# An FFN's modulation products tied to its activation products on VectorE

## The chip, the core and the metric

The kernel runs on one core of one Trainium2 chip. The metric is the device time of one execution in microseconds (us), first instruction to last and what lies around it. Three runs of the kernel before gave 2541.69 to 2549.84 us, with a median of 2549.1 us.

## What is computed

A transformer of four layers (an FFN, a mixer, an FFN each), followed by a second block of a hybrid mixer, a cross attention and one more FFN, on 256 tokens of width 1024, all in float32. The modulation of layer i is a matrix-vector product with `w_mod`, and depends on the conditioning vector alone, not on the tokens:

```python
cond = jax.nn.silu(c)
for i in range(DEPTH):                                   # DEPTH = 4
    mod = (cond @ w_mod[i] + b_mod[i]).reshape(-1, N_SUBLAYERS, N_MOD, D_MODEL)
    x = _sublayer(x, ffn_0, mod[:, 0], ...)
    x = _sublayer(x, mixer_i, mod[:, 1], ...)
    x = _sublayer(x, ffn_1, mod[:, 2], ...)

def _swiglu(h, w_in, w_out):
    gate, up = jnp.split(h @ w_in, 2, axis=-1)
    return (jax.nn.silu(gate) * up) @ w_out

def _sublayer(x, fn, mod_j, g, b, weight):
    shift, scale, gate = mod_j[:, 0, None, :], mod_j[:, 1, None, :], mod_j[:, 2, None, :]
    y = fn(x * (1 + scale) + shift)
    return _layernorm(DEEPNORM_ALPHA * x + weight * gate * y, g, b)
```

## The kernel before, in words

**A product in three matmuls.** Each float32 operand is split into a high and a low part, and a product is three matmuls: high by high, high by low, low by high. A weight arrives as a transfer of 1 MB into a `raw` tile (three of these tiles exist, `NR = 3`). ScalarE writes the high parts `whi` (L219), VectorE the low parts `wlo` in three chunks for each 128x1024 tile (L222).

**An FFN.** Its 2816 hidden columns are worked in 11 blocks (b = 0 to 10) of 256, for two halves of the tokens (t = 0, 1). FFNs are counted from 0 here; FFN 0, 2, 4, 6 are the first ones of the layers, 1, 3, 5, 7 the second ones, 8 the last of the program. The steps are:

- I(t,b): the transfer of the block's weights (three of 1 MB, at t = 0), 24 matmuls into `hid{b}t{t}`, the silu `sg` on ScalarE (L596), the activation product `ac` on VectorE (L599), and then some steps of a background generator (`tick`).
- T(t,b): two transposes of `ac` on TensorE (L263), the high part `ah` on ScalarE (L608), the low part `al` on VectorE (L609).
- O(t,b): 12 matmuls into the accumulators y0 (t = 0) or y1 (t = 1): L623 and L624 take `ah`, L625 takes `al`.

The order in which the program writes the steps of the middle blocks is I(0,b) O(0,b-1) I(1,b) T(0,b) O(1,b-1) T(1,b). After the last block, `post_ln` adds the residual and normalises y0, then y1 (L511 to L524), and what it has normalised, `r`, is transposed for the next sublayer (the L263 rows with `r`); the next sublayer's first matmuls are into `pa`, `pd` or `pz`.

**The modulation.** The background generator (`mod_dot`) computes the modulation of later sublayers: each unit of it requests 1 MB of `w_mod` into a `rawm` tile, which is one of the same three `raw` tiles, and multiplies it by the conditioning row in two VectorE instructions of 128x1024 (L364). It is called by `tick` from the FFNs' steps I in blocks 2 to 9 (26 steps in FFN 0, 2, 4, 6; 21 or 16 in the others). There are 144 such transfers and 288 products in the program.

**What sets the order.** Each engine has a queue of its own which it runs in order. A scheduler sets the order within each queue when the kernel is built: instructions are traced in the program's order and then placed by dependencies, priorities and the scheduler's own estimate of times. `tc.issue_after(x)` adds one condition for the scheduler: what is traced within it stands behind x.

Of the kernel before, what the change touches and what calls it, by code (L numbers as in the profile page):

```python
# [15 lines left out]
OP = mybir.AluOpType  # L16
# [74 lines left out]
def _ffn_order():  # L91
    o = HEAD.split()
    for b in range(2, NB - 2):
        o += [f"I0.{b}", f"O0.{b - 1}", f"I1.{b}", f"T0.{b}", f"O1.{b - 1}", f"T1.{b}"]
    a, b, c = NB - 3, NB - 2, NB - 1
    o += TAIL.format(a=a, b=b, c=c).split()
    return " ".join(o)
# [32 lines left out]
class TT:  # L130
    def __init__(self, make, n, dt, by_t):
        self.n, self.by_t = n, by_t
        if by_t is None:
            self.by_t, self.t = True, [make([P, n, P], dt)] * 2
        elif by_t:
            self.t = [make([P, n, P], dt) for _ in range(2)]
        else:
            self.t = [make([P, min(4, n - a), 2, P], dt) for a in range(0, n, 4)]
# [25 lines left out]
class Net:  # L164
    def __init__(self, ctx, tc, A, out, stop=None):
        self.tc, self.nc, self.A, self.out, self.stop = tc, tc.nc, A, out, stop
        e = ctx.enter_context
        self.cst = e(tc.tile_pool(name="cst", bufs=1))
        self.rawp = e(tc.tile_pool(name="rawp", bufs=NR))
        self.wp = e(tc.tile_pool(name="wp", bufs=NW))  # L170
        self.tp = e(tc.tile_pool(name="tp", bufs=NT))
        self.hp = e(tc.tile_pool(name="hp", bufs=NH))
        self.fp = e(tc.tile_pool(name="fp", bufs=2))
        self.sm = e(tc.tile_pool(name="sm", bufs=6))
        self.ps = e(tc.tile_pool(name="ps", bufs=2, space=bass.MemoryType.PSUM))
        self.dr = e(tc.tile_pool(name="dr", bufs=1, space=bass.MemoryType.DRAM))
        self.bg = []
        self.GB = {}
        self.pending = []
        self.late = []  # L180
        self.rs = {}
        self.n = 0
# [174 lines left out]
    def mod_dot(self, i, s, m, pv):  # L357
        nc = self.nc
        for u in range(4):
            raw = self.rawp.tile([P, 2048], F32, tag="raw", name=self.nm("rawm"))  # L360
            nc.sync.dma_start(raw, self.A["w_mod"][i, s * 3 + m, u])
            for j in range(2):
                src = raw[:, j * 1024:(j + 1) * 1024]
                nc.vector.scalar_tensor_tensor(src, src, 1.0, self.condrow, OP.mult, OP.mult,  # L364
                                               accum_out=pv[:, 2 * u + j:2 * u + j + 1])
            yield

    def bias_cols(self, i, s, m):
# [212 lines left out]
    def ffn(self, x, w_in, w_out, done, steps=0, rs=None):  # L581
        nc = self.nc
        wi, wo, act, y = {}, {}, {}, {}

        def load(b):
            wi[b] = []
            for u in range(2):
                for hi, lo in self.wload(w_in[b, u], [1024, 1024]):
                    wi[b] += [(hi, lo, 0), (hi, lo, 512)]
            wo[b] = self.wload(w_out[b], [1024, 1024])  # L590

        def first(b, t):
            ps = self.bank("mm", f"hid{b}t{t}")
            self.lin(ps, x, t, wi[b], 512)
            sg = self.fp.tile([P, 256], F32, tag="sg", name=self.nm("sg"))
            nc.scalar.activation(sg, ps[:, :256], AF.Silu, scale=1.0 if rs is None else rs[t])  # L596
            a = self.fp.tile([P, 256], F32, tag="ac", name=self.nm("ac"), bufs=NAC)
            if rs is None:
                nc.vector.tensor_tensor(a, ps[:, 256:], sg, OP.mult)  # L599
            else:  # L600
                nc.vector.scalar_tensor_tensor(a, ps[:, 256:], rs[t], sg, OP.mult, OP.mult)
            act[b, t] = a

        def turn(b, t):
            tr = self.transposes(act[b, t], 2)
            ah = self.fp.tile([P, 2, P], F32R, tag="ah", name=self.nm("ah"), bufs=NAH)
            al = self.fp.tile([P, 2, P], F32R, tag="al", name=self.nm("al"), bufs=NAH)
            nc.scalar.activation(ah, tr, AF.Copy)  # L608
            nc.vector.tensor_tensor(al, tr, ah.bitcast(F32), OP.subtract)  # L609
            act[b, t] = ah, al  # L610

        def second(b, t):
            ah, al = act.pop((b, t))
            if b == 0:
                y[t] = [self.bank("y", f"y{t}q{q}") for q in range(2)]
            order = [(k, q) for k in range(2) for q in range(2)]
            if b == NB - 1:
                order.sort(key=lambda a: a[1])
            for k, q in order:
                    hi, lo = wo[b][k]  # L620
                    f, l = b == 0 and k == 0, b == NB - 1 and k == 1
                    sl = slice(q * 512, (q + 1) * 512)
                    nc.tensor.matmul(y[t][q], ah[:, k, :], hi[:, sl], start=f, stop=False)  # L623
                    nc.tensor.matmul(y[t][q], ah[:, k, :], lo[:, sl], start=False, stop=False)  # L624
                    nc.tensor.matmul(y[t][q], al[:, k, :], hi[:, sl], start=False, stop=l)  # L625

        st = {"n": 0}

        def I(t, b):
            if b > 1 and t == 0:  # L630
                load(b)
            first(b, t)
            st["n"] += 1
            span = T_LAST - T_FIRST
            at = [max(0, min(span, m - T_FIRST)) * steps for m in (st["n"] - 1, st["n"])]
            self.tick(-(-at[1] // span) + (-at[0] // span))

        go = dict(I=I, L=load, T=lambda t, b: turn(b, t), O=lambda t, b: second(b, t))
        go.update(self.closers(y, done))
        self.go(go, _ffn_order())  # L640

    def closers(self, y, done):
        st = {}

        def D(t):
            if t:
                self.pending = done(1, y[1])
            else:
                st["fin"] = done(0, y[0])

        return {"D": D, "F": lambda: self.flush(st["fin"])}
# [937 lines left out]
```

## Time and profile before

| | |
|---|---|
| runs | 2541.69 to 2549.84 us, median 2549.1 |
| profiled execution: its time | 2548.38 us |
| its span, first to last instruction | 2546.6 us (1.8 us lie outside) |
| TensorE busy | 2471.4 us, 97% |
| VectorE busy | 2067.4 us, 81% |
| ScalarE busy | 1280.8 us, 50% |
| granted TensorE clock, mean | 0.992 |
| moved by the transfers | 235 GB/s on average |

TensorE is busy nearly all the time, and all else is read against that: time can only be saved where TensorE waits, and it is lost where TensorE has nothing queued that it can run.

### The profile page before, as it was taken

The page shows a single profiled execution, that of the slowest core. Times are in us where ns is not written, and L with a number is a line of the kernel's source. Part 1 is how long each engine was busy: PE and PEld are TensorE (multiplying, and loading weights), DVE is VectorE, ACT ScalarE, POOL GpSimd, SP SyncE. Part 2 cuts the span into 40 slices and gives each one's busy share as a digit, 9 for nine tenths or more (in the row PEclk, how much of TensorE's full clock was granted, in tenths as well). Part 3 has the DMA queues.
Part 4 walks back from the last instruction along what each step waited for, and adds up shares of the span by engine and source line. Part 5 has one row for each costly group of instructions (what it writes and reads, how often), then busy time and mean ns, then how long its engine had stood idle before and what let it go on. Part 6 is the DMA issues. An engine that isn't in the chain of part 4 may idle for free.

```text
span 2546.6 us, 34057 instructions
## 1 busy us (share of the span) xinstructions
PE 2471.4 (97%) x12024; PEld 2038.7 (80%) x12024; DVE 2067.4 (81%) x5049; ACT 1280.8 (50%) x2006; POOL 32.2 (1%) x64
## 2 busy tenths in 40 slices
PE   6999999999999999999999999999999999999998
PEld 5788778888787788788888778888878887788887
DVE  6888888889886987888889988798887756896654
ACT  4544564444456554544466544454456444555542
POOL 0000000000000000000000000000000000000000
PEclk8999999999999999999999999999999999999999
DMA  8888457868974388688742458858943764444652
GB/s 307 302 324 337 164 205 270 320 239 296 340 281 165 118 297 318 235 301 340 264 153 100 149 191 323 314 215 324 347 162 132 265 220 159 149 176 144 214 179 81
DMA packets 91866, 599.71 MB, mean 235 GB/s; under 512 B 12544, under 2 KB 14096, under 8 KB 24240
## 3 DMA queue, kind: packets, MB, share of 16 engines
q1 hardware_dynamic: 84960, 574.77, 62.1%
q0 software_dynamic: 6736, 22.78, 2.8%
q8 instruction: 94, 1.54, 0.2%
q14 instruction: 76, 0.62, 0.1%
HBM read 594.31 MB, written 3.19 MB: 235 GB/s over the span
## 4 chain that ended last, share of the span: by engine, by line
PE 81%; DVE 9%; DMA 5%; ACT 4%; issue 1%; SPq 0%; DVEq 0%; ACTq 0%
PE tr L263 3%; PE y0q L623 3%; PE y0q L625 3%; PE y0q L624 3%; DVE wlo L222 3%; PE y1q L623 3%; PE y1q L624 3%; PE y1q L625 3%; DMA rawm<-in_w_mod_dram 2%; DMA raw<-in_ffn_w_in_dram 2%; PE hid0t L254 1%; PE hid5t L254 1%; PE hid5t L252 1%; PE hid3t L254 1%; PE hid4t L252 1%; PE hid2t L254 1%
## 5 line engine op out<-in xcount | busy, mean ns | idle before, releaser
L222 DVE TENSOR_TENSOR wlo<-raw,whi 128x384 fp32r<-128x384 f32 (+1 forms) x2385 | 1082.7, 507 | 197.4 <-ACT whi L219 191.6
L219 ACT ACTIVATE whi<-raw 128x1024 fp32r<-128x1024 f32 (+1 forms) x801 | 823.0, 1051 | 426.0 <-DMA raw<-in_ffn_w_in_dram 198.6
L364 DVE SCALAR_TENSOR_TENSOR rawm<-rawm,condrow 128x1024 f32<-128x1024 f32 x288 | 341.8, 1220 | 38.3 <-DMA rawm<-in_w_mod_dram 37.3
L623 PE MATMUL y1q<-whi,ah 128*128 128x512 f32 x396 | 162.9, 411 | 4.8 <-ACT ah L608 4.8
L623 PE MATMUL y0q<-whi,ah 128*128 128x512 f32 x396 | 155.5, 393 | 0.7 <-ACT ah L608 0.2
L625 PE MATMUL y1q<-whi,al 128*128 128x512 f32 x396 | 155.6, 395 | 0.0
L625 PE MATMUL y0q<-whi,al 128*128 128x512 f32 x396 | 155.4, 393 | 0.0
L624 PE MATMUL y1q<-wlo,ah 128*128 128x512 f32 x396 | 155.1, 392 | 0.0
L624 PE MATMUL y0q<-wlo,ah 128*128 128x512 f32 x396 | 154.5, 390 | 0.0
L608 ACT ACTIVATE ah<-tr 128x256 fp32r<-128x256 f32 x198 | 74.3, 380 | 123.6 <-PE tr L263 123.5
L609 DVE TENSOR_TENSOR al<-tr,ah 128x256 fp32r<-128x256 f32 x198 | 82.0, 418 | 32.9 <-ACT ah L608 32.5
L623 PEld LDWEIGHTS y1q<-whi,ah 128*128 128x128 f32 x396 | 74.5, 188 | 19.1 <-ACT ah L608 6.7
L623 PEld LDWEIGHTS y0q<-whi,ah 128*128 128x128 f32 x396 | 74.4, 188 | 17.7 <-ACT ah L608 2.4
L625 PEld LDWEIGHTS y1q<-whi,al 128*128 128x128 f32 x396 | 74.4, 188 | 16.6
L624 PEld LDWEIGHTS y0q<-wlo,ah 128*128 128x128 f32 x396 | 74.4, 188 | 14.8
L625 PEld LDWEIGHTS y0q<-whi,al 128*128 128x128 f32 x396 | 74.3, 188 | 14.8
L624 PEld LDWEIGHTS y1q<-wlo,ah 128*128 128x128 f32 x396 | 74.9, 189 | 13.2
L285 ACT ACTIVATE ev<-tr,B,G 128x128 f32<-128x128 f32 x192 | 73.0, 465 | 21.2 <-PE tr L263 21.2
L263 PEld LDWEIGHTS tr<-k_ident,ac 128*128 128x128 f32 x396 | 53.3, 140 | 32.2 <-DVE ac L599 8.4
L263 PE MATMUL tr<-k_ident,ac 128*128 128x128 f32 x396 | 75.0, 275 | 4.2 <-DVE ac L599 4.1
L295 DVE TENSOR_TENSOR tmp<-ev,tmp 128x512 fp32r<-128x512 f32 (+1 forms) x76 | 50.7, 667 | 18.0 <-ACT tmp L287 16.4
L252 PE MATMUL hid0t<-whi,tmp 128*128 128x512 f32 x144 | 58.2, 404 | 6.1 <-ACT tmp L287 3.4
(516 smaller groups left out, 5906.7 us busy)
## 6 DMA issues: line engine op xcount, KB each, us to landing
raw<-in_ffn_w_in_dram SPq DMA_DIRECT2D x176, 1024.0 KB, 5.1
rawm<-in_w_mod_dram SPq DMA_DIRECT2D x144, 1024.0 KB, 4.9
raw<-in_ffn_w_out_dram SPq DMA_DIRECT2D x88, 1024.0 KB, 5.1
raw<-in_w_gate_up_dram SPq DMA_DIRECT2D x22, 1024.0 KB, 4.8
raw<-in_w_in_dram SPq DMA_DIRECT2D x14, 1024.0 KB, 4.8
raw<-in_diff_w_in_dram SPq DMA_DIRECT2D x12, 1024.0 KB, 4.8
raw<-in_w_down_dram SPq DMA_DIRECT2D x11, 1024.0 KB, 4.9
raw<-in_w_kv_mem_dram SPq DMA_DIRECT2D x8, 1024.0 KB, 8.6
```

The lines of the kernel that those rows point to most:

```text
L219: nc.scalar.activation(hi[:, q:e], s[:, q:e], AF.Copy)
L222: nc.vector.tensor_tensor(lo[:, q:e], s[:, q:e], hi[:, q:e].bitcast(F32), OP.subtract)
L252: nc.tensor.matmul(ps, xh, hi[:, off:off + n], start=first, stop=False)
L254: nc.tensor.matmul(ps, xl, hi[:, off:off + n], start=False, stop=last)
L263: self.nc.tensor.transpose(ps[:, j, :], src[:, j * P:(j + 1) * P], self.ident)
L285: nc.scalar.activation(src[:, j, :], ps[:, j, :], AF.Identity, scale=sc, bias=bcols[:, c + j:c + j + 1])
L364: nc.vector.scalar_tensor_tensor(src, src, 1.0, self.condrow, OP.mult, OP.mult, accum_out=pv[:, 2 * u + j:2 * u + j + 1])
L608: nc.scalar.activation(ah, tr, AF.Copy)
L609: nc.vector.tensor_tensor(al, tr, ah.bitcast(F32), OP.subtract)
L623: nc.tensor.matmul(y[t][q], ah[:, k, :], hi[:, sl], start=f, stop=False)
L624: nc.tensor.matmul(y[t][q], ah[:, k, :], lo[:, sl], start=False, stop=False)
L625: nc.tensor.matmul(y[t][q], al[:, k, :], hi[:, sl], start=False, stop=l)
```

## The change

The instruction of the activation product `ac` of the last step I is kept in `self.behind`, and the two products of a modulation unit are traced within `issue_after(self.behind)`. So they can stand in VectorE's queue only behind the activation product of the step that requests their transfer. The condition holds only in FFNs without a row scale (`rs is None`, FFN 0 to 7); it is dropped at the end of each FFN. No instruction is added or removed, and SyncE's queue, which requests the transfers, keeps its order. The new line shifts the lines behind it by 3: L364, L599, L609 and L623 to L625 of before are L367, L602, L612 and L626 to L628 now.

```diff
@@ in mod_dot
             raw = self.rawp.tile([P, 2048], F32, tag="raw", name=self.nm("rawm"))
             nc.sync.dma_start(raw, self.A["w_mod"][i, s * 3 + m, u])
-            for j in range(2):
-                src = raw[:, j * 1024:(j + 1) * 1024]
-                nc.vector.scalar_tensor_tensor(src, src, 1.0, self.condrow, OP.mult, OP.mult,
-                                               accum_out=pv[:, 2 * u + j:2 * u + j + 1])
+            with ExitStack() as st:
+                if self.behind is not None:
+                    st.enter_context(self.tc.issue_after(self.behind))
+                for j in range(2):
+                    src = raw[:, j * 1024:(j + 1) * 1024]
+                    nc.vector.scalar_tensor_tensor(src, src, 1.0, self.condrow, OP.mult, OP.mult,
+                                                   accum_out=pv[:, 2 * u + j:2 * u + j + 1])
             yield
@@ in ffn, first(b, t)
             if rs is None:
-                nc.vector.tensor_tensor(a, ps[:, 256:], sg, OP.mult)
+                self.behind = nc.vector.tensor_tensor(a, ps[:, 256:], sg, OP.mult).ins
@@ at the end of ffn
         self.go(go, _ffn_order())
+        self.behind = None
```

What this does to the queues is more than the diff says, since the scheduler places everything else anew. On VectorE, block 7 of FFN 2, from the block's first modulation product on, stood as follows before (`rawm` are the products, `ac` of `hid7t0` and `hid7t1` the activation products, `wlo` of `raw_1340` the split of block 8's weights, `sc`, `G` and `B` small sums of the modulation):

```order
L364 SCALAR_TENSOR_TENSOR rawm_1328_6380,pv_1302_6278<-rawm_1328_6380,condrow_91 128x1024 x2
L599 TENSOR_TENSOR ac_1327_6378<-hid7t0_1325_6351,sg_1326_6376 128x256
L364 SCALAR_TENSOR_TENSOR rawm_1332_6425,pv_1302_6278<-rawm_1332_6425,condrow_91 128x1024 x2
L364 SCALAR_TENSOR_TENSOR rawm_1333_6429,pv_1302_6278<-rawm_1333_6429,condrow_91 128x1024 x2
L380 TENSOR_TENSOR sc_1358_6530<-pv_1302_6278,k_b_modT_89 128x8
L386 SCALAR_TENSOR_TENSOR G_1359_6532<-sc_1358_6530,k_ln_gT_1033 128x8
L387 SCALAR_TENSOR_TENSOR B_1360_6533<-sc_1358_6530,k_ln_bT_1035 128x8
L393 TENSOR_TENSOR B_1360_6533<-B_1360_6533,k_b_modT_89 128x8
L222 TENSOR_TENSOR wlo_1342_6462<-raw_1340_6459,whi_1341_6461 128x384
L599 TENSOR_TENSOR ac_1331_6423<-hid7t1_1329_6396,sg_1330_6421 128x256
L609 TENSOR_TENSOR al_1336_6437<-tr_1334_6433,ah_1335_6436 128x256
```

The same place of the changed kernel:

```order
L602 TENSOR_TENSOR ac_1327_6378<-hid7t0_1325_6351,sg_1326_6376 128x256
L367 SCALAR_TENSOR_TENSOR rawm_1328_6380,pv_1302_6278<-rawm_1328_6380,condrow_91 128x1024 x2
L602 TENSOR_TENSOR ac_1331_6423<-hid7t1_1329_6396,sg_1330_6421 128x256
L367 SCALAR_TENSOR_TENSOR rawm_1332_6425,pv_1302_6278<-rawm_1332_6425,condrow_91 128x1024 x2
L367 SCALAR_TENSOR_TENSOR rawm_1333_6429,pv_1302_6278<-rawm_1333_6429,condrow_91 128x1024 x2
L612 TENSOR_TENSOR al_1336_6437<-tr_1334_6433,ah_1335_6436 128x256
L612 TENSOR_TENSOR al_1339_6456<-tr_1337_6452,ah_1338_6455 128x256
L383 TENSOR_TENSOR sc_1358_6530<-pv_1302_6278,k_b_modT_89 128x8
L389 SCALAR_TENSOR_TENSOR G_1359_6532<-sc_1358_6530,k_ln_gT_1033 128x8
L390 SCALAR_TENSOR_TENSOR B_1360_6533<-sc_1358_6530,k_ln_bT_1035 128x8
L396 TENSOR_TENSOR B_1360_6533<-B_1360_6533,k_b_modT_89 128x8
L222 TENSOR_TENSOR wlo_1342_6462<-raw_1340_6459,whi_1341_6461 128x384 x2
```

The products moved from ahead of `ac` to behind it, and two pairs of them (four instructions) now stand between the second `ac` and the first `al`. All of the next block's split stands behind both `al`.

On TensorE, between block 7 and block 8 of FFN 2 (behind the last matmul of `hid7t1`; `al_1309` and `ah_1308` belong to block 6, `al_1336` is the `al` of block 7 shown above), stood before the end of O(1,6), the second transposes, and then block 8:

```order
L624 MATMUL y1q1_1145_5518<-wlo_1288_6186,ah_1308_6305 128x512
L625 MATMUL y1q1_1145_5518<-whi_1287_6185,al_1309_6306 128x512
L263 MATMUL tr_1337_6452<-k_ident_81,ac_1331_6423 128x128 x2
L252 MATMUL hid8t0_1355_6501<-whi_1341_6461,tmp_1059_5120 128x512
L253 MATMUL hid8t0_1355_6501<-wlo_1342_6462,tmp_1059_5120 128x512
L254 MATMUL hid8t0_1355_6501<-whi_1341_6461,tmp_1061_5122 128x512
```

The changed kernel at the same place:

```order
L627 MATMUL y1q1_1145_5518<-wlo_1288_6186,ah_1308_6305 128x512
L628 MATMUL y1q1_1145_5518<-whi_1287_6185,al_1309_6306 128x512
L263 MATMUL tr_1337_6452<-k_ident_81,ac_1331_6423 128x128 x2
L626 MATMUL y0q0_1142_5503<-whi_1321_6339,ah_1335_6436 128x512
L627 MATMUL y0q0_1142_5503<-wlo_1322_6340,ah_1335_6436 128x512
L626 MATMUL y0q1_1143_5504<-whi_1321_6339,ah_1335_6436 128x512
L627 MATMUL y0q1_1143_5504<-wlo_1322_6340,ah_1335_6436 128x512
L626 MATMUL y1q0_1144_5517<-whi_1321_6339,ah_1338_6455 128x512
L627 MATMUL y1q0_1144_5517<-wlo_1322_6340,ah_1338_6455 128x512
L626 MATMUL y1q1_1145_5518<-whi_1321_6339,ah_1338_6455 128x512
L627 MATMUL y1q1_1145_5518<-wlo_1322_6340,ah_1338_6455 128x512
L628 MATMUL y0q0_1142_5503<-whi_1321_6339,al_1336_6437 128x512
```

The second matmuls of block 7, O(0,7) and O(1,7), which ran among block 8's, are pulled ahead of it, and the ninth row behind the second transposes takes `al_1336`. Of O(1,6), 8 matmuls are left between the first and the second transposes, where 12 stood before.

At the end of FFN 2 TensorE finished y0 before it began `hid10t1` (24 matmuls follow from here on):

```order
L623 MATMUL y0q1_1143_5504<-whi_1412_6777,ah_1418_6827 128x512
L624 MATMUL y0q1_1143_5504<-wlo_1413_6778,ah_1418_6827 128x512
L625 MATMUL y0q1_1143_5504<-whi_1412_6777,al_1419_6828 128x512
L252 MATMUL hid10t1_1434_6891<-whi_1400_6743,tmp_1060_5121 128x512
L253 MATMUL hid10t1_1434_6891<-wlo_1401_6744,tmp_1060_5121 128x512
L254 MATMUL hid10t1_1434_6891<-whi_1400_6743,tmp_1062_5123 128x512
```

Now 17 of these 24 stand ahead of y0's end, and 7 behind it:

```order
L627 MATMUL y0q1_1143_5504<-wlo_1413_6778,ah_1418_6827 128x512
L628 MATMUL y0q1_1143_5504<-whi_1412_6777,al_1419_6828 128x512
L254 MATMUL hid10t1_1434_6891<-whi_1405_6757,tmp_1062_5123 128x512
L252 MATMUL hid10t1_1434_6891<-whi_1407_6763,tmp_1060_5121 128x512
L253 MATMUL hid10t1_1434_6891<-wlo_1408_6764,tmp_1060_5121 128x512
L254 MATMUL hid10t1_1434_6891<-whi_1407_6763,tmp_1062_5123 128x512
L252 MATMUL hid10t1_1434_6891<-whi_1407_6763,tmp_1060_5121 128x512
L253 MATMUL hid10t1_1434_6891<-wlo_1408_6764,tmp_1060_5121 128x512
L254 MATMUL hid10t1_1434_6891<-whi_1407_6763,tmp_1062_5123 128x512
L626 MATMUL y1q0_1144_5517<-whi_1384_6642,ah_1421_6834 128x512
```

What follows up to the next sublayer is O(1,9) and O(1,10), 12 matmuls each, in both kernels. The eight transposes of `r` stood among the last 12 before, and stand behind all of them now. FFN 0, 4 and 6 end in the same way, with 6, 7 and 9 of the 24 left behind y0's end; FFN 1, 3, 5 and 7 end as they did.

## Rows read from the trace of the kernel before

**Rows 1.** The page: busy time by engine, and the chain that ended last by engine.

```profile
PE 2471.4 (97%) x12024; PEld 2038.7 (80%) x12024; DVE 2067.4 (81%) x5049; ACT 1280.8 (50%) x2006; POOL 32.2 (1%) x64
...
PE 81%; DVE 9%; DMA 5%; ACT 4%; issue 1%; SPq 0%; DVEq 0%; ACTq 0%
```

**Rows 2.** The page's costliest groups: busy us, mean ns, idle before and releaser.

```profile
L364 DVE SCALAR_TENSOR_TENSOR rawm<-rawm,condrow 128x1024 f32<-128x1024 f32 x288 | 341.8, 1220 | 38.3 <-DMA rawm<-in_w_mod_dram 37.3
```

**Rows 3.** Windows from block 2's to block 9's first matmul, FFN 0 to 7.

```profile
core 0: us, PE busy (x) PEld busy (x) DVE busy (x) ACT busy (x) POOL busy (x), PEclk, DMA share, GB/s
...
405.00:523.20 118.20, 118.20 (x536) 97.09 (x535) 98.98 (x218) 51.78 (x71) 2.09 (x4) 1.00 0.90 328
594.20:716.30 122.10, 120.09 (x537) 98.28 (x535) 103.83 (x228) 49.22 (x69) 3.15 (x6) 0.99 0.90 336
...
sum 952.90, PE 949.29 PEld 777.76 DVE 781.41 ACT 406.90 POOL 18.34; mean PE 118.66 PEld 97.22 DVE 97.68 ACT 50.86 POOL 2.29
```

**Rows 4.** Timeline of TensorE, FFN 2, from block 7 to block 8.

```profile
695.22 0.39 PE L625 MATMUL y1q<-whi,al 128*128 128x512 f32 x1
697.62 0.68 PE L263 MATMUL tr<-k_ident,ac 128*128 128x128 f32 x2 [2.01 <-DVE ac L599]
...
699.00 0.63 PE L254 MATMUL hid8t<-whi,tmp 128*128 128x512 f32 x1
699.43 0.63 PE L252 MATMUL hid8t<-whi,tmp 128*128 128x512 f32 x1
```

**Rows 5.** Timeline of VectorE, same place.

```profile
685.72 1.23 DVE L364 SCALAR_TENSOR_TENSOR rawm<-rawm,condrow 128x1024 f32<-128x1024 f32 x1 [2.56 <-DMA rawm<-in_w_mod_dram]
...
697.14 0.42 DVE L599 TENSOR_TENSOR ac<-hid7t,sg 128x256 f32<-128x256 f32 x1
```

**Rows 6.** Timeline of VectorE, FFN 0, block 4.

```profile
155.48 0.42 DVE L599 TENSOR_TENSOR ac<-hid4t,sg 128x256 f32<-128x256 f32 x1
...
157.83 4.87 DVE L222 TENSOR_TENSOR wlo<-raw,whi 128x384 fp32r<-128x384 f32 x11 [0.59 <-ACT whi L219]
162.62 0.42 DVE L599 TENSOR_TENSOR ac<-hid4t,sg 128x256 f32<-128x256 f32 x1
162.95 0.41 DVE L609 TENSOR_TENSOR al<-tr,ah 128x256 fp32r<-128x256 f32 x1
```

**Rows 7.** Timeline of ScalarE, same place.

```profile
153.80 0.38 ACT L596 ACTIVATE sg<-hid4t 128x256 f32<-128x256 f32 x1 [5.09 <-DVE rawm L364]
```

**Rows 8.** Timeline of TensorE, FFN 2, from y0's last matmul to the mixer's first.

```profile
744.10 0.39 PE L625 MATMUL y0q<-whi,al 128*128 128x512 f32 x1
...
749.54 0.39 PE L254 MATMUL hid10t<-whi,tmp 128*128 128x512 f32 x1
...
753.35 0.50 PE L623 MATMUL y1q<-whi,ah 128*128 128x512 f32 x1 [0.47 <-ACT ah L608]
...
754.15 0.60 PE L263 MATMUL tr<-k_ident,r 128*128 128x128 f32 x4
...
757.22 0.50 PE L252 MATMUL pd<-whi,tmp 128*128 128x512 f32 x1
```

**Rows 9.** Timeline of VectorE, same place.

```profile
753.33 0.99 DVE L518 TENSOR_SCALAR r<-r,mv,rs 128x512 f32<-128x512 f32 x2
```

**Rows 10.** Timeline of TensorE, FFN 0: y0's last matmul and the mixer's first.

```profile
261.20 0.39 PE L625 MATMUL y0q<-whi,al 128*128 128x512 f32 x1
...
274.69 0.31 PE L252 MATMUL pa<-whi,tmp 128*128 128x320 f32 x1
```

**Rows 11.** Timeline of TensorE: one wait in the mixer of layer 0.

```profile
285.68 0.56 PE L263 MATMUL tr<-k_ident,kr 128*128 128x128 f32 x2 [2.65 <-DVE kr L697]
```

**Rows 12.** Timeline of TensorE: the same wait in the mixer of layer 3.

```profile
1877.98 0.56 PE L263 MATMUL tr<-k_ident,kr 128*128 128x128 f32 x2 [2.65 <-DVE kr L697]
```

**Rows 13.** Windows of 4 us behind these two waits, columns as in rows 3.

```profile
285.60:289.60 4.00, 3.91 (x18) 2.92 (x19) 3.77 (x14) 1.38 (x3) 0.00 (x0) 1.00 0.44 151
1878.00:1882.00 4.00, 4.00 (x13) 3.24 (x14) 3.77 (x13) 0.69 (x2) 0.00 (x0) 0.58 0.51 144
```

More of the change, by code (lines that the diff above doesn't have):

```diff
@@ L176, in __init__ @@
         self.dr = e(tc.tile_pool(name="dr", bufs=1, space=bass.MemoryType.DRAM))
-        self.bg = []
+        self.bg, self.behind = [], None
         self.GB = {}
```

## The prediction

> **What bounds the kernel now.** I read the page first: TensorE is busy 97% of the span, and holds 81% of the chain that ended last; VectorE holds 9% of that chain, the transfers 5% [rows 1]. So a shorter VectorE or transfer time saves nothing by itself. Only a wait of TensorE can be won or lost, and I looked for these stage by stage.
>
> The windows view gives the FFNs, the only stages whose order the change alters. From block 2's first matmul to block 9's, seven blocks, an FFN takes 118.2 us when nothing disturbs it, and TensorE is then busy for all of it (118.20 of 118.20). All eight FFNs together take 952.9 us [rows 3], and 8 x 118.2 is 945.6. So 7.3 us is **all that the middle blocks have to give**. FFN 2 has more than half of it (122.1 - 118.2 = 3.9 us). The timeline shows that place: TensorE waits 2.01 us for an activation product, and its matmuls then come 0.43 us apart [rows 4], against 0.227 us where the clock is full (24 matmuls from 744.10 to 749.54 [rows 8]); 8 of them at this pace cost 1.6 us. VectorE had waited 2.56 us for a `rawm` transfer with the products at the head of its queue, and the activation product came at 697.14 [rows 5]. This is the wait that the change goes for. Elsewhere the products delay `ac` too, in FFN 0 by more than a microsecond (the silu starts at 153.80, lasts 0.38, and `ac` starts at 155.48 [rows 6, 7]), but TensorE has other matmuls queued there, and the block costs nothing extra.
>
> **The change, part by part.** Nothing is added or removed, so the sum is of waits that go and waits that come.
>
> *Gain.* If no product stood ahead of an activation product in a harmful place, at most the 7.3 us above would go. I credit all of it.
>
> *Cost in the blocks.* The product of a unit is 1.22 us, and there are two to a unit [rows 2]; the next starts a little before the last has ended, so a pair holds VectorE for 2.3 us. By the new order pairs stand between `ac` of t = 1 and the first `al` of the block, and TensorE has been given the block's O steps at once, which need that `al`. Call E the end of `hid{b}t1`. `sg` takes 0.38 us, `ac` 0.42, `al` 0.41 [rows 6, 7], so with n pairs between them `al` is there at E + 1.25 + 2.3n. TensorE needs it after f matmuls up to the second transposes and g behind them, at 0.227 us each, and 0.28 us for the transposes. In FFN 2, block 7, n = 2, f = 8 and g = 8: `al` at E + 5.85, needed at E + 3.9, a wait of 1.95 us. I did this sum for every block by the new order. FFN 2, 4 and 6, which have the same pattern: block 2 0.6, block 3 (n = 2, f = 8, g = 10) 1.5, block 6 0.35, block 7 1.95, block 8 0.1, that is 4.5 us each. FFN 0: 3.1 us over blocks 2 to 8, half a microsecond of it for a split that comes late in block 2. FFN 1, 3 and 5: 0.6 us each, block 6 alone. FFN 7: nothing. Together 3.1 + 3 x 4.5 + 3 x 0.6 = 18.4 us, and net of the gain **+11.1 us**. Below, this term is bounded by -7.3 (all new waits covered). Above, the next block's 18 `wlo` chunks, which before lay around `ac` (11 of them between the two, 4.87 us [rows 6]), now all follow the `al`: about 8 us of work with the block's matmuls following close behind. If this costs half a microsecond more in each of 28 blocks (seven in FFN 0, 2, 4, 6), the term is +25.
>
> What stands behind a product on VectorE does not overtake it here: in [rows 5] `ac` came only when the products queued ahead of it were through. If `al` could run ahead of the pairs, the 18.4 us would fall away and the whole sum below would be 2556.8 us in place of 2575.2. The Trainium skill says the same as a rule (TensorE: Matmul & The Clock Gate, section "Architectural detail: the array is 16× 32×32, not 1× 128×128"): the queues of VectorE and ScalarE are strictly first in, first out, and only TensorE can pull weight loads ahead. By this rule the change only exchanges what waits: before the activation product behind the pair, now the low part behind it; the trace agrees, with the 2.01 us above.
>
> *Cost at the FFN's end.* In FFN 2 y0's last matmul starts at 744.10. VectorE's post_ln chain lets `r` be normalised at 753.33, its transposes run at 754.15, and the mixer's first matmul starts at 757.22, 13.1 us after y0 [rows 8, 9]. TensorE covered that with 24 + 12 + 12 matmuls (10.9 us), two transposes of `ac` and eight of `r` (about 1 us), and waited some 1.2 us, part of it for `ah` [rows 8]. Now 17 of the 24 stand ahead of y0's end. They are work done earlier, but no longer cover: 17 x 0.227 = 3.9 us is uncovered, less what the chain gets shorter. By the new order one `wlo` chunk (0.44 us each [rows 6]) leaves the chain and one `al` (0.41) enters, so FFN 2 loses about 3.7 us, and FFN 4, whose end is like it, I take at 3.1, since less `wlo` is left in its chain. In FFN 0 the mixer starts 13.5 us after y0 [rows 10]; 18 matmuls leave the cover (4.1 us), three `wlo` chunks leave the chain and an `al` enters (-0.9): 3.2 us. FFN 6 keeps 9 of the 24: 2.5 us. Together **+12.5 us**. Bounds: 6, if half of the lost cover is given back because the mixer's start waited for something else too, and 15.2, the whole of the uncovered matmuls (18 + 17 + 17 + 15 = 67, at 0.227).
>
> *The clock.* After 2.01 us of waiting TensorE's clock was at the lower level for some 3 us [rows 4]. After two like waits of 2.65 us, in the mixers of layers 0 and 3, the granted clock was 1.00 behind one and 0.58 behind the other [rows 11 to 13]. So I take one chance in two for each of the four FFN ends, which now hold some 4 us of waiting within 8 us, at 1.6 us each: **+3.2 us**; bounds 0 and 11 (four ends and three block-7 waits).
>
> *Sum.* The profiled execution took 2548.4 us (its span of 2546.6 and 1.8 outside), 0.7 below the median of the runs. 2548.4 + 11.1 + 12.5 + 3.2 = **2575.2 us**, 1.0% above the median.
>
> **The rivals.** *Faster (one mechanism: the activation product is free).* The 7.3 us go, and the new `al` waits are covered, because TensorE reaches the O steps later than in my sum: the point is two more microseconds of matmuls between E and the first use of `al` in the blocks with n = 2. If the FFN ends lose nothing either, 2548.4 - 7.3 = 2541 us, and 2536 if their 1.2 us of waiting goes as well. For it speaks the clear 2.01 us wait for `ac` [rows 4]; against it, that `al` stands behind four products in the order, and that even this is on the edge of what can be told.
>
> *No change.* TensorE's queue covers most of what the sum counts: the blocks come out even and the ends lose a third of their 12.5 us: 2548.4 + 4 = 2552 us. For it speaks that `ac` late by a microsecond cost nothing in FFN 0 [rows 6, 7]. Against it speaks that at the ends no other work is left to put in.
>
> *Much slower: the weights come late.* A product frees a `raw` tile, and the next block's weights wait for that tile. Products that wait for `ac` free it later, so that the transfers, which are 90% busy in these windows [rows 3], have less time, and the splits follow later. If each of the 28 full blocks loses 1.5 us in place of my 0.6, 2548.4 + 42 - 7.3 + 12.5 + 3.2 = 2599 us.
>
> *The change does nothing* can be left out: the queues differ in all FFNs but the last two.
>
> **How the numbers follow.** A kernel of this spread (2541.69 to 2549.84) tells about 0.3%, 7.6 us, from no change. My forecast, slower by 10 to 40 us, has 0.66; much slower (beyond 2590) 0.12; no change 0.13; faster, with whatever of it passes 0.3%, 0.09. So slower by over 0.3% has 0.78, the same 0.14, faster 0.08. The range for 8 in 10 goes from 2551, which takes in half of the no-change case (ends at their lower bound, blocks slightly better than even), to 2599, where the splits come late.
>
> **What would show it.** Right: in FFN 2, 4, 6, block 7, TensorE waits about 2 us on `al` (L612) or on `ah` behind it; behind y0's end of FFN 0, 2, 4, 6 TensorE waits some 4 to 5 us in all for `ah`, `al`, `r` and the mixer's `tmp`; the window of seven blocks grows to about 122.5 us in FFN 2, 4, 6; VectorE's busy time stays at 2067 us. The prediction is wrong if these windows stay at 118 to 119 us, if the mixer's first matmul comes 13 us behind y0 with TensorE still busy, or if the stalls are on `whi` and `wlo` and not on `al`.

## The result, and the profile after

| | before | after |
|---|---|---|
| median of 4 runs, us | 2547.16 | 2591.31 |
| lowest to highest, us | 2541.69 to 2549.84 | 2587.2 to 2597.45 |
| profiled execution, us (its span) | 2548.4 (2546.6) | 2587.2 (2585.4) |

The changed kernel is slower: ratio 1.0168, 95% interval 1.0148 to 1.0189. The forecast was 2575 us (1.0% above), with a range of 2551 to 2599. So its direction held and its size was some 16 us short. The traces can account for 12.0 of these 16: the profiled execution after the change took 2587.2 us, 4.1 below the median of its runs.

The page of the changed kernel, with the row of busy times and that of the chain, which answer to [rows 1]:

```profile
PE 2485.5 (96%) x12024; PEld 2038.5 (79%) x12024; DVE 2062.6 (80%) x5049; ACT 1277.8 (49%) x2006; POOL 32.2 (1%) x64
...
PE 75%; DVE 13%; DMA 6%; ACT 4%; issue 2%; SPq 0%; DVEq 0%; ACTq 0%
```

VectorE does the same work in the same busy time, 2062.6 us against 2067.4, but its share of the chain that ended last went from 9% to 13%. The page's groups show both sides of the exchange:

```profile
L367 DVE SCALAR_TENSOR_TENSOR rawm<-rawm,condrow 128x1024 f32<-128x1024 f32 x288 | 338.8, 1219 | 20.0 <-DMA rawm<-in_w_mod_dram 19.7
...
L628 PE MATMUL y0q<-whi,al 128*128 128x512 f32 x396 | 155.7, 406 | 16.6 <-DVE al L612 16.6
```

VectorE's idle time ahead of the products, nearly all of it spent on their transfers, fell from 38.3 us [rows 2] to 20.0. TensorE now waits 16.6 us for the low parts `al`.

To see where the span grew (38.8 us), cut each of FFN 0 to 7 at three places: block 2's first matmul, y0's last matmul, the next sublayer's first matmul. The windows view of the first stretch, of which the last line sums the eight FFNs, first before, then after:

```profile
sum 1176.52, PE 1172.72 PEld 961.45 DVE 937.98 ACT 498.93 POOL 21.51; mean PE 146.59 PEld 120.18 DVE 117.25 ACT 62.37 POOL 2.69
```

```profile
602.88:761.05 158.17, 152.79 (x678) 123.72 (x677) 126.01 (x278) 63.86 (x88) 3.15 (x6) 0.99 0.85 313
...
sum 1223.15, PE 1198.11 PEld 971.95 DVE 937.06 ACT 502.16 POOL 21.51; mean PE 149.76 PEld 121.49 DVE 117.13 ACT 62.77 POOL 2.69
```

That is 46.6 us more. But 67 matmuls that ran behind y0's end now run ahead of it (18, 17, 17 and 15 in FFN 0, 2, 4, 6), which only moves 67 x 0.227 = 15.2 us from the second stretch to the first. **Net, the blocks lost 31.4 us.** The second stretch, y0's end to the mixer, in FFN 0, 2, 4, 6, first before, then after:

```profile
sum 53.00, PE 50.14 PEld 40.56 DVE 50.15 ACT 33.03 POOL 2.11; mean PE 12.54 PEld 10.14 DVE 12.54 ACT 8.26 POOL 0.53
```

```profile
sum 50.18, PE 36.73 PEld 27.40 DVE 47.76 ACT 25.18 POOL 2.11; mean PE 9.18 PEld 6.85 DVE 11.94 ACT 6.30 POOL 0.53
```

It is 2.8 us shorter with 15.2 us less work in it: **the ends lost 12.4 us.** All the rest of the program is 5.0 us shorter, 2.9 of it ahead of FFN 0's block 2 and 2.1 in the four mixers. The two sums and this make 38.8 us.

What TensorE waits for in the first stretch is in the waits of these eight windows, added up:

| TensorE idle, block 2 to y0, eight FFNs, us | before | after |
|---|---|---|
| for `ac` (transposes) | 3.3 | 2.9 |
| for `al` | 0 | 16.7 |
| for `whi` | 0 | 5.3 |
| all | 3.6 | 24.9 |

So 21.3 of the 31.4 us is idle time. Another 2.6, by estimate, is matmuls at half pace (0.43 us apart in place of 0.227) inside these stretches: some 4.0 us lost to them after, 1.4 before. The other 7.5 lies in matmuls that last longer just behind a wait, and in gaps too short to be listed as idle; I have not taken it further apart.

**One block in detail.** FFN 2, block 7, the place of [rows 4, 5]. TensorE after the change:

```profile
707.47 0.44 PE L263 MATMUL tr<-k_ident,ac 128*128 128x128 f32 x2 [0.62 <-DVE ac L602]
...
709.37 0.39 PE L627 MATMUL y1q<-wlo,ah 128*128 128x512 f32 x1
712.81 1.22 PE L628 MATMUL y0q<-whi,al 128*128 128x512 f32 x2 [3.05 <-DVE al L612]
713.83 0.63 PE L626 MATMUL y0q<-whi,ah 128*128 128x512 f32 x1
714.26 0.63 PE L627 MATMUL y0q<-wlo,ah 128*128 128x512 f32 x1
```

VectorE at the same place:

```profile
700.02 0.42 DVE L602 TENSOR_TENSOR ac<-hid7t,sg 128x256 f32<-128x256 f32 x1
704.70 1.23 DVE L367 SCALAR_TENSOR_TENSOR rawm<-rawm,condrow 128x1024 f32<-128x1024 f32 x1 [4.25 <-DMA rawm<-in_w_mod_dram]
...
706.99 0.42 DVE L602 TENSOR_TENSOR ac<-hid7t,sg 128x256 f32<-128x256 f32 x1
...
710.04 1.23 DVE L367 SCALAR_TENSOR_TENSOR rawm<-rawm,condrow 128x1024 f32<-128x1024 f32 x1 [0.28 <-DMA rawm<-in_w_mod_dram]
...
712.33 0.75 DVE L612 TENSOR_TENSOR al<-tr,ah 128x256 fp32r<-128x256 f32 x2
```

The first product stands behind `ac` of t = 0 at 700.02, but its transfer lands at 704.70, and `ac` of t = 1 stands behind that pair. The wait for `ac` that the change goes for is still here, 0.62 us in place of 2.01 [rows 4]. Behind that `ac` come two more pairs, and only then the two `al`. TensorE has eight matmuls for that time, and waits 3.05 us; after it the matmuls come 0.43 us apart. Before, this place cost 2.01 us and a half-pace stretch; now it costs more of both.

**Late weights.** In FFN 0 between blocks 7 and 8 another wait ends last. The chain there:

```profile
207.32 2.38 DVE rawm L367 x4
...
209.72 10.51 DMA raw<-in_ffn_w_in_dram
...
220.25 1.06 ACT whi L219
...
221.36 1.22 PE hid8t L252 x2
```

The same matmul in TensorE's timeline:

```profile
221.36 1.22 PE L252 MATMUL hid8t<-whi,tmp 128*128 128x512 f32 x2 [3.71 <-ACT whi L219]
```

A pair of products ends at 209.7 and frees its tile. The transfer of the next weights follows it, and TensorE waits 3.71 us for their high part. This is the rival "the weights come late".

**FFN 2's end**, which answers to [rows 8]; TensorE from y0's last matmul to the mixer's first:

```profile
761.05 0.39 PE L628 MATMUL y0q<-whi,al 128*128 128x512 f32 x1
...
766.45 0.50 PE L626 MATMUL y1q<-whi,ah 128*128 128x512 f32 x1 [0.47 <-ACT ah L611]
...
767.85 0.50 PE L628 MATMUL y1q<-whi,al 128*128 128x512 f32 x1 [0.20 <-DVE al L612]
...
770.74 1.08 PE L263 MATMUL tr<-k_ident,r 128*128 128x128 f32 x8 [0.79 <-DVE r L521]
773.84 0.79 PE L252 MATMUL pd<-whi,tmp 128*128 128x512 f32 x1 [2.01 <-ACT tmp L287]
```

From y0 to the mixer it is 12.8 us, against 13.1 before: the normalisation on VectorE sets this time, and the 17 matmuls that no longer run under it are not won back.

### The profile page after: what moved, and what is told of

It is laid out like the page before. It is cut to its first block, busy times and chain, and to the rows that moved or that the text cites. A ratio compares the mean times of both kernels' runs of the same rounds, so it can differ in the third digit from the quotient of the medians.

```text
span 2585.4 us, 33994 instructions
## 1 busy us (share of the span) xinstructions
PE 2485.5 (96%) x12024; PEld 2038.5 (79%) x12024; DVE 2062.6 (80%) x5049; ACT 1277.8 (49%) x2006; POOL 32.2 (1%) x64
## 4 chain that ended last, share of the span: by engine, by line
PE 75%; DVE 13%; DMA 6%; ACT 4%; issue 2%; SPq 0%; DVEq 0%; ACTq 0%
DVE wlo L222 4%; DVE rawm L367 4%; PE y0q L628 3%; DMA rawm<-in_w_mod_dram 3%; PE y0q L626 3%; PE tr L263 3%; PE y0q L627 3%; PE y1q L628 2%; PE y1q L626 2%; PE y1q L627 2%; DMA raw<-in_ffn_w_in_dram 2%; PE hid0t L254 1%; PE hid5t L253 1%; PE hid5t L254 1%; PE hid5t L252 1%
## 5 line engine op out<-in xcount | busy, mean ns | idle before, releaser
L219 ACT ACTIVATE whi<-raw 128x1024 fp32r<-128x1024 f32 (+1 forms) x801 | 817.7, 1050 | 392.9 <-DMA raw<-in_ffn_w_in_dram 150.7
L367 DVE SCALAR_TENSOR_TENSOR rawm<-rawm,condrow 128x1024 f32<-128x1024 f32 x288 | 338.8, 1219 | 20.0 <-DMA rawm<-in_w_mod_dram 19.7
L628 PE MATMUL y0q<-whi,al 128*128 128x512 f32 x396 | 155.7, 406 | 16.6 <-DVE al L612 16.6
L626 PE MATMUL y1q<-whi,ah 128*128 128x512 f32 x396 | 160.2, 405 | 4.3 <-ACT ah L611 4.3
L626 PE MATMUL y0q<-whi,ah 128*128 128x512 f32 x396 | 159.6, 403 | 0.7 <-ACT ah L611 0.2
L628 PE MATMUL y1q<-whi,al 128*128 128x512 f32 x396 | 153.4, 397 | 0.2 <-DVE al L612 0.2
L628 PEld LDWEIGHTS y0q<-whi,al 128*128 128x128 f32 x396 | 73.6, 191 | 41.2 <-DVE al L612 27.7
L612 DVE TENSOR_TENSOR al<-tr,ah 128x256 fp32r<-128x256 f32 x198 | 79.3, 418 | 29.5 <-ACT ah L611 29.2
L626 PEld LDWEIGHTS y1q<-whi,ah 128*128 128x128 f32 x396 | 74.4, 188 | 20.2 <-ACT ah L611 6.4
L626 PEld LDWEIGHTS y0q<-whi,ah 128*128 128x128 f32 x396 | 75.3, 190 | 16.0 <-ACT ah L611 2.4
L628 PEld LDWEIGHTS y1q<-whi,al 128*128 128x128 f32 x396 | 73.1, 188 | 16.0 <-DVE al L612 1.1
```

Source lines behind the costliest of these rows:

```text
L219: nc.scalar.activation(hi[:, q:e], s[:, q:e], AF.Copy)
```

## The experiments

Each diff is against the changed kernel. Ratios are to the kernel before, run on the same chip.

**1. TensorE's order put back.** `pinned` wraps each I, T and O step of an FFN from block 2 on, and ties it behind the one before:

```diff
+        pin = {"on": rs is None, "last": None}
...
+                with ExitStack() as e:
+                    if pin["last"] is not None:
+                        e.enter_context(self.tc.issue_after(pin["last"]))
+                    pin["last"] = f(t, b)
```

> The changed kernel with TensorE's steps of each FFN (block 2 on) tied to the order of before (I0.b O0.b-1 I1.b T0.b O1.b-1 T1.b); VectorE keeps nearly the changed order: the products behind `ac`, the next block's split behind the products and both `al`. Theory A (the products behind `ac` are what costs, because the low parts and the next split come late; the pulled-forward O steps are only how the scheduler fills that time): the FFN ends are as before, so the 12.4 us there go, but the next block's first low part is ready at about E + 2.1 + 2.3n and needed at E + 3.5 (E the end of hid t1, n the pairs behind its `ac`): 1.0 us for n = 1, 3.2 or more for n = 2, in FFN 0, 2, 4, 6 some 13 us each, in FFN 1, 3, 5 some 3: 2547 + 61 = 2608 us, waits of TensorE on `wlo`. Theory B (the new order of TensorE is what costs, the place of the products is harmless): back to before, 2545 to 2555 us.

Measured: 2681.66 us, ratio 1.0505 (1.0472 to 1.0538). B is out. The waits are those of theory A, on `wlo`, but the loss is twice the 61 us that A gave. From the waits of this kernel:

```profile
ACT whi L219 <- DMA raw<-in_ffn_w_in_dram: 277.9, 70, 7.7
...
PE hid3t L253 <- DVE wlo L222: 18.6, 7, 4.2
...
PE hid4t L253 <- DVE wlo L222: 14.2, 8, 3.2
```

TensorE's waits for `wlo` add up to 76 us in blocks 3 to 10, those for `whi` to 19. The products in their new place delay the splits of the next weights. (ScalarE's wait for these weights, the first line, was 198.6 us before and 150.7 in the changed kernel; it does not follow the loss.) The O steps that the scheduler pulled forward are what softens that in the changed kernel: TensorE does them while the weights come. The new order on TensorE is a remedy, not a cause.

**2. The cover at the FFN's end put back.** `hid10t1` is tied behind y0's last matmul:

```diff
+            with ExitStack() as e:
+                if t and b == NB - 1 and rs is None:
+                    e.enter_context(self.tc.issue_after(st["y"]))
+                first(b, t)
```

> The changed kernel with one tie more: `hid10t1` stands behind y0's end on TensorE, as before, so that 24 matmuls cover the post_ln chain again. Theory A (the 17 matmuls taken out of the cover cost 12.4 us at the four FFN ends, apart from the rest): 2591 - 12 = 2579 us, blocks as in the changed kernel. Theory B (the ends only give back what was worked ahead; y0 comes later by the same time): 2591 us, and y0's end comes 4 us sooner while the mixer's start does not.

Measured: 2594.68 us, ratio 1.0161 (1.0131 to 1.0192): nothing gained, theory B. The ends are back to what they cost before (y0 to the mixer 13.39 us in FFN 2, with all 24 matmuls under it), but the blocks lose as much more: from block 9's first matmul to y0's end FFN 0, 2, 4, 6 take 115.7 us, against 118.5 in the changed kernel less the 15.2 of the moved matmuls, which is 12.4 us more. In FFN 2, just ahead of y0's end, TensorE now waits here:

```profile
762.73 0.66 PE L263 MATMUL tr<-k_ident,ac 128*128 128x128 f32 x4 [0.93 <-DVE ac L602]
...
764.44 0.50 PE L626 MATMUL y0q<-whi,ah 128*128 128x512 f32 x1 [1.05 <-ACT ah L611]
```

So the 12.4 us at the ends are not a separate cost. In the kernel before, the O steps run one block behind, a store of 24 matmuls. The changed order spends that store in the middle blocks, and block 10 then has to wait for its own `ac`, `ah` and `al`, either there or behind y0.

**3. The products of t = 1 behind the first `al`.** The units of I(1,b) are requested in T(0,b) and tied to its `al`:

```diff
+            if st.get("due"):
+                if rs is None:
+                    self.behind = i
+                self.tick(st.pop("due"))
```

> The changed kernel, but the units of step I(1,b) are traced in T(0,b) and tied to the first `al` of the block, so that no product stands between the second `ac` and the first `al`; the second `al` and the next split still stand behind them. Theory A (TensorE's waits on the first `al`, about 21 us in all, come from the pairs ahead of it): these go, the second `al` has 12 matmuls (2.7 us) more cover, and a few us come at the ends, where 3 matmuls more leave the cover: 2575 to 2580 us. Theory B (VectorE has too much to do between `ac` and the next split wherever the products stand): 2588 to 2595 us, with the waits moved to the second `al` and to `whi` and `wlo`.

Measured: 2580.71 us, ratio 1.0102 (1.0063 to 1.0141). Theory A: 0.66% of the 1.68% comes back, some 17 us. The waits for y0's `al` are gone, and in their place there is a smaller one for the second `al`:

```profile
PE y1q L632 <- DVE al L612: 7.9, 4, 2.9
```

**4. The tie one step looser.** The products are tied to the `ac` of the step before the one that requests them:

```diff
-                self.behind = nc.vector.tensor_tensor(a, ps[:, 256:], sg, OP.mult).ins
+                self.behind = self.ahead
+                self.ahead = nc.vector.tensor_tensor(a, ps[:, 256:], sg, OP.mult).ins
```

> The products tied to the activation product of the step before the one that requests their transfer. TensorE's order is that of before but for 52 places, VectorE's but for 376. Theory A (a tie costs only where it pushes products behind an `ac` whose `al` or next split TensorE waits for): 2547 us, within 5. Theory B (any tie that delays products makes the weights' transfers late): 2555 us or more, FFN 0, 2, 4, 6 longer by 2 us each.

Measured: 2550.8 us, ratio 0.999 (0.9973 to 1.0008), theory A: with one step more of freedom nothing is lost. A gain of the few us that the blocks hold is not seen either, but the interval, which reaches 6.9 us below the kernel before, cannot exclude it.

**5. Products of half the length.** The tie stays, each product works 512 of its 1024 columns (so half of every modulation sum is left out). The scheduler keeps the O steps pulled forward, but not the whole order: in block 7 of FFN 0, 2, 4 and 6 one pair is left between the second `ac` and the first `al`, where the changed kernel has two:

```diff
-                    src = raw[:, j * 1024:(j + 1) * 1024]
+                    src = raw[:, j * 1024:j * 1024 + 512]
```

> The changed kernel with products over 512 of the 1024 columns of each half unit (half of each modulation sum is left out; the transfers stay whole), so that a pair holds VectorE for about 1.2 us in place of 2.3. TensorE's order is like that of the changed kernel: O steps pulled forward, FFN ends with 28 or 30 matmuls of cover. Theory A (the loss comes from the time that pairs hold VectorE behind `ac`, ahead of `al` and the next split): the waits on `al` fall from 21 us to some 5, what follows late falls with them, the ends keep about 13: ratio to before about 1.008. Theory B (the loss comes from the order of TensorE and the later release of the raw tiles, not from the products' length): ratio 1.014 to 1.017 as in the changed kernel.

Measured: 2574.47 us, ratio 1.0114 (1.0072 to 1.0157), between the two theories; the interval takes in A's 1.008 and B's 1.014, so the run does not decide. Its profiled execution (2593.76) is some 19 us above its other three (2573.4 to 2575.02, about 1.009), so I read no sizes from its trace, beyond that TensorE's waits for `al` are 3.1 us there, where A gave some 5. By the median a third of the loss goes with the length of the products (nearly half by those three runs), and the rest does not.

**6. The tie in FFN 1, 3, 5, 7 alone.**

```diff
-                self.behind = nc.vector.tensor_tensor(a, ps[:, 256:], sg, OP.mult).ins
+                ac = nc.vector.tensor_tensor(a, ps[:, 256:], sg, OP.mult).ins
+                self.behind = ac if steps < 26 else None
```

> The tie only in FFN 1, 3, 5 and 7 (16 or 21 background steps each, in place of 26); FFN 0, 2, 4, 6 as before, with TensorE's order at their ends as before. Theory A (the loss of each FFN is its own and grows with the pairs behind its activation products): 5 us, what these FFNs lost in the changed kernel's trace (1.2, 1.8, 2.0): ratio 1.002. Theory B (the loss is a matter of the whole schedule): some other share, over 1.005.

Measured: 2552.56 us, ratio 1.0014 (1.0 to 1.0028), theory A: nearly all of the loss is in FFN 0, 2, 4, 6, where 26 units are requested and the blocks hold more products.

**7 and 8. One half of the tie each.** In 7 only the products requested in I(1,b) are tied, in 8 (`t == 0` in the last line) only those of I(0,b):

```diff
-                self.behind = nc.vector.tensor_tensor(a, ps[:, 256:], sg, OP.mult).ins
+                ac = nc.vector.tensor_tensor(a, ps[:, 256:], sg, OP.mult).ins
+                self.behind = ac if t == 1 else None
```

> Only the units requested by the steps I(1,b) are tied to their activation product; those of I(0,b) are free. The scheduler gives nearly the changed order, but for block 2. Theory A (the pairs behind the second `ac` of a block do the harm): nearly all of the loss, ratio 1.014 to 1.017. Theory B (both ties count alike): half, 1.008.

> Only the units requested by the steps I(0,b) are tied; those of I(1,b) are free, and half of their products move ahead of the second `ac`. No whole pair stands between the second `ac` and the first `al` more than once in a block. Theory A: the waits on the first `al` go nearly all, the next split is still behind most products and the ends are as in the changed kernel: ratio 1.005 to 1.009. Theory B (both ties count alike): 1.008; so this run tells A and B apart only with the one before it. Theory C (the O steps that are pulled forward cost by themselves): 1.015.

Measured: 7 took 2582.13 us, ratio 1.0125 (1.0096 to 1.0154); 8 took 2573.47 us, ratio 1.0093 (1.0062 to 1.0124). For 7, B's 1.008 is out, and A's 1.014 lies in the interval; for 8, theory C (1.015) is out, and A and B are not told apart. By the medians each half alone costs more than half of the whole (for 8 the interval also allows less), and together (1.25 + 0.93%) they would give more than the 1.68% measured. The parts seem to share a reserve, and are not terms to be added. The wait for `al` belongs to the products of t = 1: kernel 8's list of waits has none of TensorE for `al`, kernel 7's has this:

```profile
PE y0q L629 <- DVE al L613: 13.3, 11, 4.1
```

**9. All products behind the `al` of their own step.** The units of I(t,b) are requested in T(t,b) and tied to its `al`, so none stands between an `ac` and the `al` made from it:

```diff
-            nc.vector.tensor_tensor(al, tr, ah.bitcast(F32), OP.subtract)
+            self.behind = nc.vector.tensor_tensor(al, tr, ah.bitcast(F32), OP.subtract).ins
             act[b, t] = ah, al
+            self.tick(st.get((b, t), 0))
```

> The units of step I(t,b) are requested in T(t,b) and tied to that step's own low part `al`, so that no product of a step can stand between an `ac` and the `al` made from it; the transfers are requested later by that, too. Theory A (the loss is the place of the products between `ac` and `al`, and any place outside it is harmless): the waits on `al` go from the top of the list, ratio to the kernel before 0.998 to 1.004. Theory B (whatever has to wait for a product on VectorE inside a block costs, since there is no slack behind `al` either: the next block's low parts `wlo` follow there): the waits come back on `wlo` and on the `ac` of the next step, ratio 1.008 to 1.02.

Measured: 2717.08 us, ratio 1.0646 (1.0627 to 1.0664). Theory A is out. B has the direction, but neither its size nor its place. TensorE's idle time is 101 us longer than before (2715.5 - 2539.3 against 2546.6 - 2471.4 us), and the largest part of that, some 43 us, are waits for `whi`, behind the transfers. The chain in FFN 2, between blocks 2 and 3:

```profile
655.36 0.42 DVE al L612
655.77 2.47 DVE rawm L367 x5
...
659.12 1.23 DVE rawm L367 x3
660.37 6.17 DMA raw<-in_ffn_w_in_dram
666.57 1.06 ACT whi L219
667.66 1.04 DVE wlo L222 x2
668.74 0.79 PE hid3t L253
```

TensorE at the same place:

```profile
667.68 0.73 PE L252 MATMUL hid3t<-whi,tmp 128*128 128x512 f32 x2 [4.38 <-ACT whi L219]
```

A product that ends at 660.3 frees a `raw` tile; the weights for block 3 go into it and land 6.2 us later; TensorE begins block 3 after 4.38 us of waiting. In the whole kernel ScalarE waits 287.1 us for these weights. VectorE's busy time is 2065.4 us, about as before. The edit requests the `w_mod` transfers later, too, so that SyncE's order changes with VectorE's; the run does not tell apart what each of the two costs. The Trainium skill (Perfetto Trace Analysis, section "Identifying Performance Opportunities") says that kernels in general improve by improving the most contended engine. The trace agrees as far as that engine is TensorE, 97% busy before against VectorE's 81% [rows 1], and 101 us of the loss are its idle time; but no busy time shows where these waits come from, since VectorE's changed by 2.0 us only.

**10. The tie two steps looser.** As 4, with the `ac` of two steps back:

```diff
+                self.behind, self.ahead = self.ahead[0], [self.ahead[1], nc.vector.tensor_tensor(a, ps[:, 256:], sg, OP.mult).ins]
```

> The products are tied to the `ac` of two steps back (one block earlier, the same t), so that the tie holds them back only where the scheduler would have put them a whole block early. Theory A (the loss of the change comes from how far the products are pushed back, and none is left one step back already): ratio 0.997 to 1.002, like the kernel tied one step back. Theory B (some of the up to 8 us that the blocks hold in the kernel before can be won by a looser tie): 0.994 to 0.997.

Measured: 2550.99 us, ratio 1.0004 (0.9986 to 1.0022). On all five engines this kernel's instructions stand exactly in the order of the kernel before: the tie binds nothing any more. So it tests neither theory, and shows instead what the measurement makes of two equal programs. Their medians agree, but a single wait does not. TensorE's waits for `ac` in the whole program, first in the profiled execution of the kernel before, then in this one:

```profile
PE tr L263 <- DVE ac L599: 4.1, 6, 2.0
```

```profile
PE tr L263 <- DVE ac L602: 10.3, 7, 3.0
```

So a change of a few us in these waits cannot be read from one execution of each kernel.

A fourth `raw` tile, which might take the late weights away and leave the products where they are, has no room in the memory of this kernel, so no run shows what it would do.

## Why the forecast held, and where it fell short

- **"Only a wait of TensorE can be won or lost."** Held. VectorE's busy time is within 5 us in the kernels before, after, 1 and 9, and the time differs by up to 170 us.
- **The forecast's main case, slower by 10 to 40 us.** The median lies 44 us above that of the kernel before, and 1.3 us inside the case "much slower (beyond 2590)", which had 0.12. That case was built on late weights, and it was not they that brought the time there: they cost 5.3 us.
- **The gain, 7.3 us credited whole.** This step failed in the profiled executions. TensorE's idle time for `ac` went from 3.3 to 2.9 us. The place that the forecast was read from shows why: the first pair of the block waits for its own transfer and `ac` of t = 1 stands behind it (706.99, behind the transfer of 704.70). The change moved products behind one `ac`, and so nearer to the next one. The size is less sure, since the two equal programs of experiment 10 differ by 6.2 us in these waits; kernel 4 shows no gain from a looser tie, within its interval.
- **The cost in the blocks, 18.4 us of waits for `al`.** Held in size and in place: 16.7 us of idle time in 17 waits, 1.6 us in FFN 0 (forecast 3.1), 4.8, 4.1 and 4.1 in FFN 2, 4, 6 (4.5 each), 0.3, 0.9 and 0.9 in FFN 1, 3, 5 (0.6 each). Within FFN 2, 4, 6 two errors offset each other: block 7 waits longer than forecast (3.05, 2.68 and 2.67 us against 1.95), the other blocks less. In block 7 of FFN 2 the sum E + 5.85 came 2.1 us too early (E is 704.78, `al` is there at 712.75), chiefly because it let `ac` of t = 1 come without delay; TensorE was late as well, by 1.1 us, so 1.95 us became 3.05. Kernels 3, 7 and 8 show that this wait belongs to the products of t = 1.
- **Late weights.** Named as a rival at 1.5 us in each of 28 blocks, and priced at nothing in the sum. They cost 5.3 us in three places, chiefly FFN 0's block 8. Kernels 1 and 9 show that late splits and late weights are real and large once the products go further back or TensorE may not fill the time; in the changed kernel the O steps pulled forward keep them small.
- **Net in the blocks: +11.1 forecast, +31.4 measured.** This is the term that was mis-sized, by 20.3 us: 6.6 of the 7.3 of gain did not come (idle time other than for `al` and `whi` fell by 0.7 alone), 5.3 are late weights, 2.6 half-pace matmuls inside the blocks and 7.5 what stands behind the waits, for all of which the sum had nothing, less 1.7 that the waits for `al` came out shorter. It lies above the upper bound of +25.
- **The ends, +12.5 forecast, +12.4 measured** (3.2, 3.5, 3.1 and 2.6 us in FFN 0, 2, 4, 6, against 3.2, 3.7, 3.1 and 2.5). TensorE's waits behind y0's end are 3.1 to 3.8 us in each, where the forecast had 4 to 5. The working was right, and the cause only half: kernel 2 put the cover back and gained nothing, since the loss moves into block 10. It is the end of the store of O steps, wherever that shows.
- **The clock, +3.2 forecast.** All four ends, not two, fell to the lower level. The windows of 4.1 us from the mixer's first matmul in FFN 2, before and after, with the clock as the third column from the right:

```profile
757.12:761.22 4.10, 4.00 (x17) 2.91 (x17) 4.04 (x7) 4.08 (x8) 0.00 (x0) 1.00 0.70 265
```

```profile
773.74:777.84 4.10, 4.00 (x11) 3.20 (x12) 3.83 (x7) 4.08 (x8) 0.00 (x0) 0.58 0.52 216
```

  Yet the four mixers together took 2.1 us less than before, not more, so the lost clock cannot be seen in their length. In the mixers of layers 0 and 3 a part of it stands where TensorE waited before: the two waits of 2.65 us for `kr` [rows 11, 12] are shorter now:

```profile
293.58 0.56 PE L263 MATMUL tr<-k_ident,kr 128*128 128x128 f32 x2 [1.46 <-DVE kr L701]
...
1918.15 0.56 PE L263 MATMUL tr<-k_ident,kr 128*128 128x128 f32 x2 [1.37 <-DVE kr L701]
```

- **Windows of seven blocks: 122.5 us forecast, 128.5 to 128.9 measured** in FFN 2, 4, 6. Nine or ten of the matmuls pulled forward lie in them (546 or 547 records, against 537 in [rows 3]), some 2 us; the rest is waits, larger than forecast by the terms above.
- **The products are not overtaken.** The sum let `al` wait for every pair ahead of it, and it did (707.38 to 712.33). The rule of the Trainium skill quoted in the prediction agrees with that.

That the measured time lies in the range is in part luck. The term of the blocks lay above its own upper bound, and was offset by 3.2 us of clock that did not show, 5.0 us less elsewhere and 0.1 at the ends: 20.3 - 8.3 = 12.0 us.

What stays open: how the 7.5 us behind the waits divide, and why 5.0 us went elsewhere in the program, 2.9 of it before anything that the change moves has run. Two executions of one kernel differ by as much: the kernel of experiment 10, equal to the one before, reaches block 2 of FFN 0 at 110.51, 3.3 us sooner than it (113.83). The division of the loss rests on one execution of each kernel, and its small terms are no surer than that.

## What to carry to other kernels

To move work back in the queue of an engine that is not the bound, ask of each place what stands behind it there, and when the work's own buffer comes free: here the first made TensorE wait for `al`, and the second made it wait for weights in kernel 9. A gain that is a wait removed should be credited only after the new queue has been followed to the next instruction of the same kind, since the wait may just move to it. Terms read at several places that draw on one store of ready work, as the O steps here, do not add up: undo one alone, and the loss shows in another.

## What was not expected of the hardware

After waits of 2.0 us at the four FFN ends, the granted clock over the next 4.1 us was 0.58 to 0.68, but after a wait of 2.65 us in a mixer of the kernel before it was 1.00 [rows 11, 13]. In block 7 of FFN 2 the 3.05 us wait was followed by a granted clock of 0.50 for 2.8 us, the lower of the two levels, 1.2 GHz. The same wait in block 7 of FFN 4 and FFN 6 lasted 2.68 and 2.67 us; the next 2.8 us after it:

```profile
1228.90:1231.70 2.80, 2.80 (x12) 2.34 (x13) 2.73 (x10) 2.33 (x3) 0.00 (x0) 1.00 1.01 424
1845.53:1848.33 2.80, 2.80 (x7) 2.23 (x8) 1.54 (x7) 1.88 (x2) 0.00 (x0) 0.52 1.00 401
```

One kept 2.4 GHz, the other fell to 1.2. The length of a wait alone does not tell whether the clock falls.
